# One over the root mean square by a single power instruction on GpSimd in a two-layer attention encoder

## The chip, the cores and the metric

The kernel runs on one core of one Trainium2 chip. The metric is the device time of one execution in microseconds (us). Before the change it is 863.17 us, the median of three runs (861.14 to 863.44).

## What is computed

The reference runs two layers over 512 tokens of 1024 features, in float32. Each layer normalises its input by the root mean square, projects it, mixes tokens by attention, multiplies by a gate and projects back onto the residual. What matters here is the normalisation, which is used in two forms: over the 1024 features of a token, and over the 64 features of each head of q and k.

```python
def rms_norm(x, g):
    xf = x.astype(jnp.float32)
    y = xf * lax.rsqrt(jnp.mean(xf * xf, axis=-1, keepdims=True) + RMS_EPS)
    return (y * g.astype(jnp.float32)).astype(x.dtype)

# layer A (dilated windows), for each of 3 groups:
q = rms_norm(qkv[:, :, g, 0], q_gain[g]); k = rms_norm(qkv[:, :, g, 1], k_gain[g])
# layer B (neighbourhood on a grid):
q = rms_norm(q.reshape(b, s, N_HEADS, HEAD_DIM), q_gain) * (HEAD_DIM ** -0.5)
k = rms_norm(k.reshape(b, s, N_HEADS, HEAD_DIM), k_gain)
```

So every place needs `(mean + eps) ** -0.5`, for 4 values per partition (tokens) or 16 or 32 values per partition (heads of a tile of tokens).

## The kernel before, in words

**Work and order.** The 16 heads are handled in 8 pairs (`hc` 0 to 7), first for layer A, then for layer B, with an output projection after each layer. Weights stream from HBM in tiles of 512 or 384 columns. Every weight tile is split into a high part `wh` (a cast on ScalarE, `split`, L127) and a low part `wl` (a subtraction, L131, on VectorE for three tiles of five and on GpSimd for two of five, L128 to L131). TensorE then makes three matmuls for each product: high by high, high by low, low by high. A tile's halves have four buffers each and are made up to four tiles ahead. TensorE's instructions stand in a hand-written order: the main sequence of projections (`main`) is mixed with a side sequence (`side`) of attention work by a clock that adds up the length of the matmuls, and waits such as `yield "wait", ("rawq", hc), 15000` say how much later than the projection the transposes of q may come. The order on the other engines is found by the framework's scheduler from its own simulated times; each engine runs its instructions strictly in that order.

**The norm of the heads.** In layer A the projection of k for two groups gives `rawk` (four token tiles of 512 columns, of which 256 are k: 16 heads' sums per partition) and that of q gives `rawq` (four token tiles of 512 columns, three groups of q and one of k: 32 sums per partition). In layer B one projection gives q, k and v at once (16 sums per partition). Each token tile is evicted from PSUM by ScalarE with the token's factor `rs_n` (L428), squared on GpSimd (`squares`, L268) and summed on VectorE (L269). Then `head_norm` calls `rsqrt`, on VectorE when there are 32 sums (q of layer A, 8 times) and on GpSimd when there are 16 (k of layer A and all of layer B, 16 times). The result `rs` multiplies the tile on VectorE (L284, four instructions). This scaling is issued at once for k of layer A and for q of its last two pairs; in the other cases it is held back in `later` until after the gate's first multiplication (`gate_a` L458, `main_b` L899). After it TensorE transposes q and k (L210).

**The norm of the tokens.** `row_scale` calls `rsqrt` on VectorE with 4 sums per partition, which come from PSUM, once in each layer. The result `rs_n` is the scale of the evictions that follow and is spread over a tile by TensorE (`spread`).

**`rsqrt`.** It works out `v = ss * scale + EPS` (L108), makes a first guess of the inverse root by integer arithmetic on the bits (L109), and takes three Newton steps. On VectorE a step has three instructions (L113, L115, L116), on GpSimd four (L113, L118, L119, L120). So a call has 11 instructions on VectorE and 14 on GpSimd. The buffer `v` has one instance, `a` two.

Of the kernel before, what the change touches and what calls it, by code (L numbers as in the profile page):

```python
# [13 lines left out]
F32 = mybir.dt.float32  # L14
F32R = mybir.dt.float32r
I32 = mybir.dt.int32
AF = mybir.ActivationFunctionType
ALU = mybir.AluOpType
# [4 lines left out]
P = 128  # L23
# [19 lines left out]
def tile_hybrid_encoder(  # L43
# [13 lines left out]
    nc = tc.nc  # L57
    ctx.enter_context(tc.manual_schedule(engines={mybir.EngineType.PE}))

    cp = ctx.enter_context(tc.tile_pool(name="cp", bufs=1))  # L60
    big = ctx.enter_context(tc.tile_pool(name="big", bufs=1))
    wp = ctx.enter_context(tc.tile_pool(name="wp", bufs=3))
    wk = ctx.enter_context(tc.tile_pool(name="wk", bufs=2))
# [31 lines left out]
    lb_d = dr.tile([P, 376], F32, name="lb_d")  # L95
    gb_d = dr.tile([P, 248], F32, name="gb_d")

    v0 = [cp.tile([P, 4, P], F32, name=f"v0_{i}") for i in range(2)]

    hn_h = big.tile([P, KT, S], F32R, name="hn_h")  # L100
# [2 lines left out]
    y_l = big.tile([P, KT, S], F32R, name="y_l")  # L103

    def rsqrt(eng, r, ss, n, scale):
        v = wk.tile([P, 32], F32, tag="nv", name="nv", bufs=1)
        a = wk.tile([P, 32], F32, tag="na", name="na")
        eng.tensor_scalar(v[:, :n], ss, scale, EPS, op0=ALU.mult, op1=ALU.add)  # L108
        eng.tensor_scalar(  # L109
            r.bitcast(I32), v[:, :n].bitcast(I32), -0.5, float(0x5F3759DF), op0=ALU.mult, op1=ALU.add  # L110
        )
        for _ in range(3):
            eng.tensor_mul(a[:, :n], r, r)  # L113
            if eng is nc.vector:
                eng.scalar_tensor_tensor(a[:, :n], a[:, :n], -0.5, v[:, :n], op0=ALU.mult, op1=ALU.mult)  # L115
                eng.scalar_tensor_tensor(r, a[:, :n], 1.5, r, op0=ALU.add, op1=ALU.mult)  # L116
                continue
            eng.tensor_mul(a[:, :n], a[:, :n], v[:, :n])  # L118
            eng.tensor_scalar(a[:, :n], a[:, :n], -0.5, 1.5, op0=ALU.mult, op1=ALU.add)  # L119
            eng.tensor_mul(r, r, a[:, :n])  # L120

    turn, pool = [0], [2, 5]

# [151 lines left out]
    def head_norm(raw, ss, ns, held):  # L275


        rs = wk.tile([P, 32], F32, tag="rs", name="rs")
        rsqrt(nc.vector if ns == 8 else nc.gpsimd, rs[:, : 4 * ns], ss[:, : 4 * ns], 4 * ns, 1.0 / DH)

        def scale():
            for i in range(4):
                v = raw[:, i, : ns * 64].rearrange("p (a b) -> p a b", b=64)
                m = nc.vector.tensor_mul(  # L284
                    v, v, rs[:, i * ns : (i + 1) * ns].unsqueeze(2).to_broadcast([P, ns, 64])
                )
                if held:
                    tc.keep_in_program_order(m)

        if held:  # L290
            later.append(scale)
        else:
            scale()
# [33 lines left out]
    def row_scale(ssq):  # L327

        rsqrt(nc.vector, rs_n, ssq, 4, 1.0 / D)
# [854 lines left out]
```

## Time and profile before

| | before |
|---|---|
| median of 3 runs | 863.17 us |
| the profiled execution | 863.44 us |
| its span, first to last instruction | 861.7 us |
| TensorE clock granted | 0.999 |
| DMA, mean over the span | 149 GB/s |
| ScalarE (ACT) busy | 423.1 us (49%) |
| L284, the scaling of q and k on VectorE, with `rawq` | 32 instructions, median 684 ns |
| L428, the eviction of `rawq` on ScalarE | 32 instructions, median 690 ns |

A profile row of a group names the line of the kernel, the engine, the operation, what it writes and reads, and its count, then its busy time in us and the mean of one in ns, and then the idle time of its engine ahead of it with what ended that idle time. PE is TensorE, PEld its loading of weights, DVE VectorE, ACT ScalarE, POOL GpSimd, SP the engine that issues the DMAs. In a view by tile the three durations are the shortest, the median and the longest in ns. In a timeline the first column is the start in us from the beginning of the span, the second the duration in us.

### The profile page before, as it was taken

The numbers are of one execution on the slowest core, as the hardware profiler recorded it, in microseconds if no ns is written. First come the engines' busy times: TensorE is split into PE (matmuls) and PEld (weight loads), VectorE is DVE, ScalarE is ACT, GpSimd is POOL, SyncE is SP. The second block draws the span as 40 slices with busy tenths as digits, with TensorE's granted clock in tenths as the row PEclk, the third lists the DMA queues.
The fourth block names the chain that finished last, engine by engine and source line by source line (L and its number), as shares of the span: only waits on it lengthen the run. The fifth ranks groups of instructions, "written<-read, shape, count | busy, mean of one in ns | idle before, by whom it ended". The sixth has DMA issues, their size and how long they took to land.

```text
span 861.7 us, 15492 instructions
## 1 busy us (share of the span) xinstructions
PE 854.2 (99%) x5643; PEld 712.2 (83%) x5643; DVE 513.3 (60%) x1323; ACT 423.1 (49%) x880; POOL 296.2 (34%) x493
## 2 busy tenths in 40 slices
PE   8999999999999999999999999999999999999998
PEld 6788888788788788788788788789988899889786
DVE  6445666566476566566466775538466656766642
ACT  7432653553553553553552564435466645665541
POOL 2351441441541432442342432112444335542411
PEclk9999999999999999999999999999999999999999
DMA  7343565564465464465465274265235664656223
GB/s 247 110 131 108 150 170 157 159 178 137 138 202 156 125 200 130 133 192 148 129 171 175 84 229 105 65 197 179 95 113 149 180 168 145 167 160 174 99 96 124
DMA packets 59707, 128.64 MB, mean 149 GB/s; under 512 B 6384, under 2 KB 23728, under 8 KB 59632
## 3 DMA queue, kind: packets, MB, share of 16 engines
q1 hardware_dynamic: 59344, 127.66, 49.3%
q8 instruction: 44, 0.72, 0.4%
q14 instruction: 31, 0.25, 0.1%
q10 hardware_dynamic: 288, 0.01, 0.0%
HBM read 102.82 MB, written 24.83 MB: 148 GB/s over the span
## 4 chain that ended last, share of the span: by engine, by line
PE 97%; ACT 1%; DVE 1%; DMA 1%; issue 0%; ACTq 0%; DVEq 0%
PE acc L206 82%; PE log L206 5%; PE o L206 5%; PE tp L210 4%; DMA hg<-in_head_gain 1%; ACT p L976 1%; DVE hn_l L368 0%; ACT p L564 0%; ACT rawk L428 0%; ACT wh L127 0%; PE pa L206 0%; PE pl L206 0%; PE pk L206 0%; DVE wl L131 0%; DVE pt L889 0%
## 5 line engine op out<-in xcount | busy, mean ns | idle before, releaser
L127 ACT CAST wh<-wraw 128x512 fp32r<-128x512 f32 (+1 forms) x276 | 161.6, 587 | 298.1 <-PE acc L206 247.4
L206 PE MATMUL acc<-wh,hn_h 128*128 128x512 f32 (+1 forms) x768 | 296.5, 386 | 0.8 <-ACT wh L127 0.7
L206 PE MATMUL acc<-wh,hn_l 128*128 128x512 f32 (+1 forms) x768 | 286.6, 373 | 0.0
L206 PE MATMUL acc<-wl,hn_h 128*128 128x512 f32 (+1 forms) x768 | 286.1, 373 | 0.4 <-DVE wl L131 0.4
L131 POOL TENSOR_TENSOR wl<-wraw,wh 128x512 fp32r<-128x512 f32 (+1 forms) x110 | 137.7, 1252 | 392.9 <-ACT wh L127 342.2
L131 DVE TENSOR_TENSOR wl<-wraw,wh 128x512 fp32r<-128x512 f32 (+1 forms) x166 | 113.2, 682 | 141.5 <-ACT wh L127 137.0
L206 PEld LDWEIGHTS acc<-wh,hn_h 128*128 128x128 f32 x768 | 144.6, 188 | 27.4 <-issue 5.5
L206 PEld LDWEIGHTS acc<-wh,hn_l 128*128 128x128 f32 x768 | 144.6, 188 | 21.1
L206 PEld LDWEIGHTS acc<-wl,hn_h 128*128 128x128 f32 x768 | 144.9, 189 | 19.0 <-DVE wl L131 0.9
L206 PE MATMUL acc<-hn_h,wh 128*128 128x512 f32 x192 | 76.9, 400 | 0.2
L206 PE MATMUL acc<-hn_h,wl 128*128 128x512 f32 x192 | 74.9, 390 | 0.0
L206 PE MATMUL acc<-hn_l,wh 128*128 128x512 f32 x192 | 74.8, 390 | 0.0
L725 ACT ACTIVATE p<-p,mn 128x512 f32<-128x512 f32 (+1 forms) x64 | 44.8, 700 | 53.9 <-DVE mn L714 53.9
L564 ACT ACTIVATE p<-p,mn 128x512 f32<-128x512 f32 (+3 forms) x128 | 69.1, 586 | 0.0
L269 DVE TENSOR_REDUCE ss<-sq 128x4 f32<-128x256 f32 (+1 forms) x96 | 48.4, 504 | 27.3 <-POOL sq L268 26.8
L636 DVE STREAM_TRANSPOSE tr<-p 128x512 f32<-128x512 f32 (+1 forms) x80 | 54.1, 688 | 12.1 <-ACT p L564 10.0
L268 POOL TENSOR_TENSOR sq<-rawk 128x256 f32<-128x256 f32 x64 | 40.5, 640 | 40.5 <-ACT rawk L428 33.5
L206 PE MATMUL acc<-y_h,wh 128*128 128x512 f32 x128 | 52.2, 408 | 0.0
L206 PE MATMUL acc<-y_h,wl 128*128 128x512 f32 x128 | 50.0, 390 | 0.0
L206 PE MATMUL acc<-y_l,wh 128*128 128x512 f32 x128 | 50.0, 390 | 0.0
L206 PEld LDWEIGHTS acc<-hn_h,wh 128*128 128x128 f32 x192 | 36.1, 188 | 9.8 <-ACT rawk L428 2.1
L206 PEld LDWEIGHTS acc<-hn_h,wl 128*128 128x128 f32 x192 | 36.0, 188 | 7.7
(131 smaller groups left out, 1077.8 us busy)
## 6 DMA issues: line engine op xcount, KB each, us to landing
wraw<-in_w SPq DMA_DIRECT2D x95, 512.0 KB
wraw<-in_w SPq DMA_DIRECT2D x38, 384.0 KB
td<-tr SPq DMA_DIRECT2D x56, 256.0 KB
pt<-td SPq DMA_DIRECT2D x56, 256.0 KB
td<-tr SPq DMA_DIRECT2D x24, 224.0 KB
pt<-td SPq DMA_DIRECT2D x24, 224.0 KB
e<-l_d SPq DMA_DIRECT2D x32, 112.0 KB
e<-l_d SPq DMA_DIRECT2D x16, 128.0 KB
```

The source lines that it names most:

```text
L127: nc.scalar.copy(h, raw)
L131: eng.tensor_sub(l, raw, h.bitcast(F32))
L206: nc.tensor.matmul(o, l, r, **kw)
L210: nc.tensor.transpose(o, i, ident)
L268: nc.gpsimd.tensor_mul(sq, raw[:, i, : ns * 64], raw[:, i, : ns * 64])
L269: nc.vector.tensor_reduce(ss[:, i * ns : (i + 1) * ns], sq.rearrange("p (a b) -> p a b", b=64), axis=AX.X, op=ALU.add)
L564: nc.scalar.activation(pr, pr, AF.Copy, scale=mn[:, 3:4])
L636: nc.vector.transpose(dst, src[:, :n].rearrange("p (i b k) -> p i b k", b=4, k=32))
L725: nc.scalar.activation(row, row, AF.Exp, bias=mn[:, 1:2], scale=-1.0, accum_out=mn[:, 2:3])
L976: nc.scalar.activation(pr[:, o : o + n], pr[:, o : o + n], AF.Exp, bias=mn[:, 0:1], scale=-1.0, accum_out=mn[:, 2:3])
```

## The change

`rsqrt` keeps its first instruction on the engine that it had (VectorE or GpSimd). The guess and the Newton steps go, and one instruction takes their place, on GpSimd in all 26 calls: a tensor raised to the power that a second tensor holds, which is a constant tile of -0.5. That tile is filled once at the start by VectorE. The buffer `a` goes, and `v` has two instances now.

```diff
+    neg = cp.tile([P, 32], F32, name="neg")
+    nc.vector.memset(neg, -0.5)
...
     def rsqrt(eng, r, ss, n, scale):
-        v = wk.tile([P, 32], F32, tag="nv", name="nv", bufs=1)
-        a = wk.tile([P, 32], F32, tag="na", name="na")
+        v = wk.tile([P, 32], F32, tag="nv", name="nv")
         eng.tensor_scalar(v[:, :n], ss, scale, EPS, op0=ALU.mult, op1=ALU.add)
-        eng.tensor_scalar(
-            r.bitcast(I32), v[:, :n].bitcast(I32), -0.5, float(0x5F3759DF), op0=ALU.mult, op1=ALU.add
-        )
-        for _ in range(3):
-            eng.tensor_mul(a[:, :n], r, r)
-            if eng is nc.vector:
-                eng.scalar_tensor_tensor(a[:, :n], a[:, :n], -0.5, v[:, :n], op0=ALU.mult, op1=ALU.mult)
-                eng.scalar_tensor_tensor(r, a[:, :n], 1.5, r, op0=ALU.add, op1=ALU.mult)
-                continue
-            eng.tensor_mul(a[:, :n], a[:, :n], v[:, :n])
-            eng.tensor_scalar(a[:, :n], a[:, :n], -0.5, 1.5, op0=ALU.mult, op1=ALU.add)
-            eng.tensor_mul(r, r, a[:, :n])
+        nc.gpsimd.tensor_tensor(r, v[:, :n], neg[:, :n], op=ALU.pow)
```

## The prediction, made before the result was known

> **What bounds the kernel.** I read the page's head first, then the chain that ended last, then the waits of TensorE.
>
> ```profile
> span 861.7 us, 15492 instructions
> PE 854.2 (99%) x5643; PEld 712.2 (83%) x5643; DVE 513.3 (60%) x1323; ACT 423.1 (49%) x880; POOL 296.2 (34%) x493
> ...
> PE 97%; ACT 1%; DVE 1%; DMA 1%; issue 0%; ACTq 0%; DVEq 0%
> ```
>
> TensorE is busy for 854.2 of 861.7 us and 97% of the last chain is its own. So 7.5 us at most could be had by making other engines quicker. The view of the waits, asked for TensorE alone, says how much of that ended with a late producer:
>
> ```profile
> PE busy L346 <- DVE warm L335: 1.5, 1, 1.5
> PE acc L206 <- ACT wh L127: 0.7, 1, 0.7
> PE acc L206 <- DVE wl L131: 0.4, 1, 0.4
> PE tp L210 <- ACT p L564: 0.4, 1, 0.4
> PE o L206 <- issue: 0.3, 1, 0.3
> ```
>
> None of the rows names `rs` or `rs_n`. The norm is therefore off the path now, and the whole question is how late its result may become before TensorE stands still for it.
>
> **What goes.** The view by tile of `na` shows the removed steps (shortest/median/longest in ns):
>
> ```profile
> L113 POOL TENSOR_TENSOR na<-rs x48: 216/217/667, 44.4 to 804.0; 128x16 f32<-128x16 f32 x48
> L118 POOL TENSOR_TENSOR na<-na,nv x48: 217/223/550, 44.7 to 804.3; 128x16 f32<-128x16 f32 x48
> L119 POOL TENSOR_SCALAR na<-na x48: 203/205/688, 45.0 to 804.6; 128x16 f32<-128x16 f32 x48
> L120 POOL TENSOR_TENSOR rs<-rs,na x48: 222/223/768, 45.3 to 804.9; 128x16 f32<-128x16 f32 x48
> L115 DVE SCALAR_TENSOR_TENSOR na<-na,nv x30: 155/192/1271, 36.3 to 604.5; 128x32 f32<-128x32 f32 x24, 128x4 f32<-128x4 f32 x6
> ```
>
> On GpSimd 16 calls lose 13 of their 14 instructions, 192 of them in these rows: 48 x (217+223+205+223) ns = 41.7 us busy at the medians. On VectorE 8 calls lose ten instructions of about 0.19 us each, some 15 us at the medians, and two calls ten shorter ones. Neither engine is the bound (60% and 34% busy), so this time is worth nothing by itself.
>
> **What comes: the price of the power.** The trace has no power instruction. The nearest below is a GpSimd multiplication of the same size, 217 ns for 16 columns (L113). The nearest in width is this row of the view by tile of `sq`:
>
> ```profile
> L268 POOL TENSOR_TENSOR sq<-rawq x32: 1032/1042/1061, 55.3 to 488.2; 128x512 f32<-128x512 f32 x32
> ```
>
> From 16 to 512 columns the time grows by 825 ns, that is 1.66 ns a column, and 0.19 us stay fixed. A power needs a logarithm, a product and an exponential. I count some 80 elementary steps (an estimate from the arithmetic, no row shows it). Three prices follow:
> - floor: 0.22 us for 16 columns, as one multiplication; with the columns' growth 0.25 us for 32;
> - chosen: 80 steps at 1.66 ns, 0.133 us a column with 0.19 us fixed: 0.7 us for 4 columns, 2.3 us for 16, 4.4 us for 32;
> - ceiling: every step costs as much per column as a whole separate instruction of 16 columns does, 217/16 = 13.6 ns: 1.09 us a column, 17.5 us for 16 and 34.9 us for 32.
>
> I take the middle value because the power is one instruction whose steps run without a start between them, so that the wide row is the nearer one. The choice is weak, and the ends lie far apart.
>
> **Where it stands: q of layer A (8 calls, 32 columns).** Timelines of VectorE, GpSimd and TensorE around pair 1:
>
> ```profile
> 126.10 0.22 DVE L108 TENSOR_SCALAR nv<-ss 128x32 f32<-128x32 f32 x1
> ...
> 128.16 1.27 DVE L115 SCALAR_TENSOR_TENSOR na<-na,nv 128x32 f32<-128x32 f32 x1
> 129.46 0.19 DVE L116 SCALAR_TENSOR_TENSOR rs<-na,rs 128x32 f32<-128x32 f32 x1
> 130.34 0.69 DVE L458 TENSOR_TENSOR gt<-acc,rs_half 128x512 f32<-128x512 f32 x1 [0.68 <-PE acc L206]
> 130.94 2.49 DVE L284 TENSOR_TENSOR rawq<-rawq,rs 128x512 f32<-128x512 f32 x4
> ...
> 128.09 1.29 POOL L131 TENSOR_TENSOR wl<-wraw,wh 128x512 fp32r<-128x512 f32 x1 [1.81 <-ACT wh L127]
> ...
> 135.58 0.60 PE L210 MATMUL tp<-ident,rawq 128*128 128x128 f32 x4
> 136.25 0.40 PE L206 MATMUL acc<-wl,hn_h 128*128 128x512 f32 x1
> ```
>
> Now `rs` is ready at 129.65, but the scaling is held behind the gate's product until 130.94 and takes 2.49 us, and TensorE transposes at 135.58. `rs` may thus come as late as 135.58 - 2.49 = 133.09. With the change the first instruction ends at 126.32, some 0.1 us pass on the way to the other engine (as between 604.87 and 604.96 in a fence below; taken between the two instructions everywhere), and the power runs from 126.42 to 130.8: still ahead of 130.94. The cover is 133.09 - 126.42 = 6.7 us, so this place turns at a price of 0.2 us a column. What queues behind the power is the GpSimd subtraction of 128.09, moved to 130.8 and ended by 132.1, against its use by TensorE at 136.25: also covered. In pair 6 the scaling isn't held back, and less is covered:
>
> ```profile
> 456.17 0.22 DVE L108 TENSOR_SCALAR nv<-ss 128x32 f32<-128x32 f32 x1
> ...
> 459.75 2.50 DVE L284 TENSOR_TENSOR rawq<-rawq,rs 128x512 f32<-128x512 f32 x4
> ...
> 463.61 0.60 PE L210 MATMUL tp<-ident,rawq 128*128 128x128 f32 x4
> ```
>
> Here 463.61 - 2.50 - 456.49 = 4.6 us are covered, just over the 4.4 us that I take. VectorE waits there with the scaling in its queue, and its next subtraction follows 1.1 us later.
>
> The row of 1.27 us above is a step whose median is 0.19 us: it began while the GpSimd subtraction of 128.09 ran, and ended with it. So a VectorE instruction with two inputs in SBUF stands still while GpSimd reads. The Trainium skill says the same in "SBUF — State Buffer", section "SBUF: two separate sides": the pair of ports that the two engines share is locked for a whole instruction. The trace agrees (0.19 became 1.27 us). By that rule a power of 4.4 us blocks VectorE's two-input work for all of it. In pair 1 only the gate's product stands there, and one of its inputs is in PSUM, so the sum stays; it speaks against the change only where the power is long.
>
> **k of layer A and layer B (16 calls, 16 columns).** Timelines of k in pair 1, then of pair 2 in layer B:
>
> ```profile
> 96.91 0.21 POOL L108 TENSOR_SCALAR nv<-ss 128x16 f32<-128x16 f32 x1 [0.96 <-DVE ss L269]
> ...
> 97.97 1.29 POOL L131 TENSOR_TENSOR wl<-wraw,wh 128x512 fp32r<-128x512 f32 x1
> ...
> 102.68 1.43 DVE L284 TENSOR_TENSOR rawk<-rawk,rs 128x256 f32<-128x256 f32 x4 [1.30 <-POOL rs L120]
> ...
> 107.65 0.39 PE L206 MATMUL acc<-wl,hn_h 128*128 128x512 f32 x1
> 112.19 0.38 PE L210 MATMUL tp<-ident,rawk 128*128 128x128 f32 x2
> ```
>
> ```profile
> 662.73 0.20 POOL L108 TENSOR_SCALAR nv<-ss 128x16 f32<-128x16 f32 x1
> ...
> 668.73 2.23 DVE L284 TENSOR_TENSOR rawk<-rawk,rs 128x256 f32<-128x256 f32 x4 [0.72 <-POOL rs L120]
> ...
> 671.91 0.60 PE L210 MATMUL tp<-ident,rawk 128*128 128x128 f32 x4
> ```
>
> In both the chain of 14 steps lasts nearly 6 us, because a subtraction or a `y_l` slips in between its steps. With the power it lasts 0.3 + 2.3 = 2.6 us, about 3 us less, and VectorE's waits of 1.30 and 0.72 us for `rs` go. TensorE gains nothing: its transposes come at their place in the order. The covers are 112.19 - 1.43 - 97.2 = 13.5 us for k, 107.65 - 1.29 - 97.2 = 9.1 us for the subtraction that queues behind the power, and 671.91 - 2.23 - 663.03 = 6.65 us in layer B.
>
> **The tokens' norm (2 calls, 4 columns) and the constant.** At the start of layer B:
>
> ```profile
> 601.87 0.16 DVE L108 TENSOR_SCALAR nv<-pk 128x4 f32<-128x4 f32 x1 [1.48 <-PE pk L206]
> ...
> 604.71 0.16 DVE L116 SCALAR_TENSOR_TENSOR rs_n<-na,rs_n 128x4 f32<-128x4 f32 x1
> 604.96 2.00 ACT L428 ACTIVATE rawk<-acc,rs_n 128x384 f32<-128x384 f32 x4 [0.31 <-DVE rs_n L116]
> ```
>
> The chain of 3.0 us becomes 0.16 + 0.1 + 0.7 us, or some 2 us if a GpSimd subtraction of 1.3 us is ahead of it. This brings the evictions forward by about 1 us, ahead of matmuls that already run. I count nothing. The constant is one small fill at the start, while TensorE only waits for its first weights: nothing.
>
> **Sum.** Zero on the path, with perhaps half a microsecond of the small waits recovered: 863.4 - 0.2 = 863.2 us, from the profiled execution's 863.44 us (span 861.7 and 1.7 around it), which is also about the median of the runs, 863.17.
>
> **Rivals.**
> 1. *The power is slow* because its steps wait for one another. Its prices begin at 0.2 us a column, where q of pair 1 starts to lose (1.5 times what I chose), and end here at 0.38, the geometric mean of my price and the ceiling. At that end a power takes 6.3 us for 16 columns and 12.35 for 32. Layer B and k stay covered (6.65, 9.1). q loses 12.35 - 6.67 = 5.7 us in seven pairs (0 and 7 taken like pair 1) and 7.7 in pair 6: 47.5 us, 911 us at the far end, 866 to 911 for the case. For it: 80 steps that need each other's results sit in one instruction. Against it: the wide multiplication shows no such cost, though its columns don't need each other. The Trainium skill, "GPSIMD Engine Reference", section "Performance pitfalls for Q7 kernels", prices a dependent float32 chain at 4 cycles an element on the chain; no run here shows it. At the page's 1.2 GHz an estimate from it is 80 x 4 cycles = 0.27 us a column, 8.7 us for 32 columns, and 7 x 2.1 + 4.1 = 19 us, 882 us.
> 2. *Dearer than that, up to the ceiling*, as if the values were taken one after another: at the ceiling q loses 7 x 28.2 + 30.3 = 228 us, k 8 x (17.5 - 9.1) = 67 by the subtraction behind it, layer B 8 x 10.85 = 87: 382 us, 1245 us. For it: the trace shows no power at all. Against it: no GpSimd row here pays anew for every column.
> 3. *A new wait in GpSimd's queue at my price*: if the power of q is ordered behind the subtraction of 128.09, which itself waits for ScalarE, it ends at 129.4 + 4.4 = 133.8, 0.7 us too late, in seven pairs; in pair 6 3.0 us too late. 8 us, 871 us. It decides once that subtraction comes first. For it: GpSimd was idle for 1.81 us ahead of it, so the order is open. Against it: the power is ready 1.7 us before it.
> 4. *Faster*: the waits of the rows above that could end, 0.7 + 0.4 + 0.4 us, go: 861.9 us. More than 0.3% (2.6 us) would need a third of all TensorE's idle time.
>
> **Chances.** My forecast 0.44, rival 1 0.27, rival 2 0.15, rival 3 0.10, rival 4 0.04. 0.3% is about what a measurement of this kernel can tell from no change. So: faster 0.04, within 0.3% 0.44, slower 0.52. The slower ones together hold more than the forecast, which is only the likeliest single case; its own range is 861 to 866. The range of 861 to 912 adds rivals 1 and 3 and leaves out rival 2 and the ends of the others, some 2 in 10.
>
> **What would show it.** Right: a power of about 2.3 us for 16 columns and 4.4 us for 32, twice what 16 take but for the fixed part; the scaling of q starting after the gate's product as now; no row of TensorE waiting for VectorE's `rawq`. VectorE's busy time falls by some 20 us, and GpSimd's rises by some 28: 16 x 2.3 + 8 x 4.4 + 2 x 0.7 = 73 us come, 45 go with guess and steps. Wrong: a power over 6.7 us for 32 columns, with idle TensorE ahead of the transposes of `rawq` in each pair of layer A, then of layer B, or GpSimd's `wl` late.

## The result, and the profile after

The changed kernel takes 873.06 us (median, 872.62 to 875.25), against 862.75 us for the kernel before on the same chip. The ratio is 1.0127 with a 95% interval from 1.0104 to 1.015: slower by 9 to 13 us. The time lies in the range that was given, but not where the forecast put it.

The head of the page of the kernel after, and the chain that ended last:

```profile
span 870.9 us, 15207 instructions
PE 857.4 (98%) x5643; PEld 712.7 (82%) x5643; DVE 503.2 (58%) x1224; ACT 424.1 (49%) x880; POOL 338.2 (39%) x311
...
PE 90%; DVE 5%; ACT 2%; DMA 2%; POOL 1%; issue 1%; ACTq 0%; SPq 0%; DVEq 0%; POOLq 0%
```

The chain, 97% TensorE before, now runs for 5% of the span over VectorE. The waits of TensorE in the kernel after say where:

```profile
PE tp L201 <- DVE rawq L275: 4.5, 13, 1.3
PE tp L201 <- DVE mn L705: 2.2, 1, 2.2
```

Both rows are new: the transposes of q (L201, L210 before) wait for the scaling of q (L275, L284 before) 13 times, and once for the softmax. In the view by tile of `nv` stands what could not be seen before, the power itself:

```profile
L111 POOL TENSOR_TENSOR rs<-nv,neg x24: 2898/2902/5458, 42.3 to 810.5; 128x16 f32<-128x16 f32 x16, 128x32 f32<-128x32 f32 x8
L111 POOL TENSOR_TENSOR rs_n<-nv,neg x2: 1014/1020/1026, 34.1 to 612.5; 128x4 f32<-128x4 f32 x2
```

It takes 1.02 us for 4 columns, 2.90 for 16 and about 5.44 for 32: 0.16 us a column and some 0.38 us fixed.

TensorE's 5643 matmuls stand in the same order in all kernels here, so the start of each can be set against its start in the kernel before. The table has how much later TensorE is after each stretch than ahead of it, from the profiled executions, in us. "Pair" is the attention of that pair of heads in layer A.

| kernel | pair 0 | pairs 1 to 5, each | pair 6 | pair 7 | rest |
|---|---|---|---|---|---|
| after | 0.0 | 0.92 to 0.94 | 2.77 | 3.99 | -0.1 |
| e1_newton_q | 0.0 | 0.0 | 0.0 | -0.1 | -0.3 |
| e2_pow_q_only | 0.0 | 0.95 to 1.25 | 4.34 | 2.38 | -0.3 |
| e3_moved | 0.0 | 0.0 | 0.60 | 1.31 | -0.2 |
| e4_newton_pool | 0.0 | 0.0 | 0.61 | 1.76 | -0.4 |
| e5_moved_twice | 6.40 | 5.7 to 5.8 | 7.86 | 7.49 | 0.1 |
| e6_pieces | 0.7 | 0.0 | 0.52 | 1.56 | 0.6 |
| e7_before_moved | 0.0 | 0.0 | 0.0 | 0.0 | -0.1 |

All of the loss is at q of layer A, in pairs 1 to 7: 11.4 us by the sum of the row. The first 30 us are left out of the table, since they differ from execution to execution: the kernel after is 1.87 us earlier there than the profiled execution of before, and so is e4_newton_pool, which has no power, by 1.91 us. That is why the spans differ by 9.2 us only. A row is one execution; that of e4_newton_pool was its fastest of five (863.27 us, median 865.05).

Pair 1 in the timelines of the kernel after, VectorE first, then GpSimd, then TensorE:

```profile
124.22 0.22 DVE L110 TENSOR_SCALAR nv<-ss 128x32 f32<-128x32 f32 x1
128.45 0.69 DVE L449 TENSOR_TENSOR gt<-acc,rs_half 128x512 f32<-128x512 f32 x1 [4.01 <-PE acc L197]
129.06 0.68 DVE L122 TENSOR_TENSOR wl<-wraw,wh 128x512 fp32r<-128x512 f32 x1
...
130.18 4.69 DVE L275 TENSOR_TENSOR rawq<-rawq,rs 128x512 f32<-128x512 f32 x4
...
124.52 5.44 POOL L111 TENSOR_TENSOR rs<-nv,neg 128x32 f32<-128x32 f32 x1
129.92 1.50 POOL L122 TENSOR_TENSOR wl<-wraw,wh 128x512 fp32r<-128x512 f32 x1
131.91 1.81 POOL L122 TENSOR_TENSOR wl<-wraw,wh 128x512 fp32r<-128x512 f32 x1 [0.49 <-ACT wh L118]
...
133.69 0.38 PE L201 MATMUL tp<-ident,rawq 128*128 128x128 f32 x2
134.33 0.33 PE L201 MATMUL tp<-ident,rawq 128*128 128x128 f32 x1 [0.25 <-DVE rawq L275]
134.93 0.33 PE L201 MATMUL tp<-ident,rawq 128*128 128x128 f32 x1 [0.28 <-DVE rawq L275]
```

The power ends at 129.96, and the scaling starts at 130.18, 3.51 us ahead of the first transpose, where it was 4.64 us ahead before (135.58 - 130.94). After scalings of 2.49 us there were 2.15 us left over; the power's length takes 1.1 of them, and the rest would do. But the four scalings last 4.69 us where they lasted 2.49. While the power ran, a GpSimd subtraction became due (ScalarE's cast for it began at 125.50) and had to wait; it starts at 129.92, the next follows at 131.91, and both run while q is scaled. Only the first of them was held up. In the kernel before, the second is this row:

```profile
133.80 1.38 POOL L131 TENSOR_TENSOR wl<-wraw,wh 128x512 fp32r<-128x512 f32 x1 [4.42 <-ACT wh L127]
```

It starts 1.78 us ahead of the first transpose there (135.58 - 133.80) and in the kernel after (133.69 - 131.91). Before, the scaling was over by then; now it runs later and into it. Each of the two stretches the scaling that it meets. The view by tile of `rawq` has the longest one:

```profile
L275 DVE TENSOR_TENSOR rawq<-rawq,rs x32: 677/680/1787, 66.9 to 504.9; 128x512 f32<-128x512 f32 x32
```

Two of four scalings take 1.78 us instead of 0.68: 2.2 us more. With the 1.1 us of above that is more than was left over, by 1.2 us. The last scaling is needed only by the fourth transpose, so 0.9 us are lost. Of the 2.15 us, the lateness alone leaves about half, and the collisions alone would leave about nothing (an estimate from these rows): by it the loss takes both together.

### The profile page after: what moved, and what is told of

It reads as the page before. It is cut to its first block, busy times and chain, and to the rows that moved or that the text cites. A ratio compares the mean times of both kernels' runs of the same rounds, so it can differ in the third digit from the quotient of the medians.

```text
span 870.9 us, 15207 instructions
## 1 busy us (share of the span) xinstructions
PE 857.4 (98%) x5643; PEld 712.7 (82%) x5643; DVE 503.2 (58%) x1224; ACT 424.1 (49%) x880; POOL 338.2 (39%) x311
## 4 chain that ended last, share of the span: by engine, by line
PE 90%; DVE 5%; ACT 2%; DMA 2%; POOL 1%; issue 1%; ACTq 0%; SPq 0%; DVEq 0%; POOLq 0%
PE acc L197 75%; PE log L197 5%; PE o L197 5%; PE tp L201 4%; DVE rawq L275 3%; POOL rs L111 1%; DMA td<-tr 1%; DMA pt<-td 1%; ACT p L967 1%; DMA hg<-in_head_gain 0%; DVE gt L449 0%; DVE hn_l L359 0%; ACT eg L452 0%; ACT p L555 0%; ACT rawk L419 0%
## 5 line engine op out<-in xcount | busy, mean ns | idle before, releaser
L122 POOL TENSOR_TENSOR wl<-wraw,wh 128x512 fp32r<-128x512 f32 (+1 forms) x110 | 140.3, 1275 | 387.5 <-ACT wh L118 323.4
L111 POOL TENSOR_TENSOR rs<-nv,neg 128x16 f32<-128x16 f32 (+1 forms) x24 | 90.2, 3759 | 4.0 <-DVE nv L110 1.9
L275 DVE TENSOR_TENSOR rawk<-rawk,rs 128x256 f32<-128x256 f32 x64 | 33.1, 577 | 20.1 <-POOL rs L111 20.1
```

The lines of the kernel that those rows point to most:

```text
L111: nc.gpsimd.tensor_tensor(r, v[:, :n], neg[:, :n], op=ALU.pow)
L122: eng.tensor_sub(l, raw, h.bitcast(F32))
L275: m = nc.vector.tensor_mul(v, v, rs[:, i * ns : (i + 1) * ns].unsqueeze(2).to_broadcast([P, ns, 64]))
```

## The experiments

Theory A: the power of q ends in time, or nearly, but it pushes two GpSimd subtractions into the scaling of q, and the ports that the two engines share do the damage. (By the rows above it pushes one, and the later scaling runs into the other.) Theory B: the power is simply late for q. Theory C: long instructions in GpSimd's queue cost everywhere. Theories D, L and M came with later runs and are told there.

**Newton steps for q alone.** The edit to the kernel before, in `rsqrt`, besides the constant tile (the guess and the Newton steps stay below it; `v` and `a` have one buffer each):

```diff
-        a = wk.tile([P, 32], F32, tag="na", name="na")
         eng.tensor_scalar(v[:, :n], ss, scale, EPS, op0=ALU.mult, op1=ALU.add)
+        if n < 32:
+            nc.gpsimd.tensor_tensor(r, v[:, :n], neg[:, :n], op=ALU.pow)
+            return
+        a = wk.tile([P, 32], F32, tag="na", name="na", bufs=1)
```

> The power stays for k of layer A, for layer B and for the tokens (16 and 4 columns); q of layer A (32 columns) has its Newton steps on VectorE back. Theory A (the power of q ends in time, but pushes two GpSimd subtractions into the scaling of q, where the shared ports stretch it): the whole loss goes, 861 to 865 us, ratio to before 0.998 to 1.002, scaling of q 2.5 us for four. Theory B (the power itself is late for q): the same here, 861 to 865. Theory C (any long instruction in GpSimd's queue costs, whatever its size): the 16 remaining powers of 2.9 us keep half of the loss or more, 867 to 870.

Measured: 861.17 us against 861.87, ratio 0.9996 (0.9986 to 1.0005). The 16 powers for k and for layer B, and the two for the tokens, cost nothing and bring nothing. Theory C falls.

**The power for q alone.** The same edit with `if n == 32`.

> The power for q of layer A alone; all other places keep guess and Newton steps. Theories A and B: the whole loss is here, 871 to 875 us, with about 0.96 us lost in each of pairs 1 to 5 and 2.5 to 4 in pairs 6 and 7. Theory C: a third to a half of it, 866 to 869.

Measured: 874.43 us, ratio 1.0138 (1.0122 to 1.0154). The whole loss is here, with nearly the same share in each of pairs 1 to 5. Pair 6 loses more than was expected (4.34 us) and pair 7 less (2.38), where the kernel after has 2.77 and 3.99. Two rows of a view by windows, one behind the transposes of each pair, show why (after the stretch: its length, the busy times of PE, PEld, DVE, ACT and POOL, then the granted clock of TensorE):

```profile
472.30:475.80 3.50, 3.50 (x12) 2.81 (x11) 0.81 (x2) 0.96 (x2) 0.00 (x0) 0.51 0.00 0
511.20:513.20 2.00, 2.00 (x13) 1.78 (x14) 1.90 (x10) 2.00 (x6) 0.00 (x0) 1.00 0.06 17
```

Behind pair 6 the clock is at half, which costs 1.6 us against the kernel after (4.34 - 2.77); behind pair 7 it stays at 1.00. In the kernel after it is pair 7 that meets the half clock, as is shown further down.

**The subtractions out of the way.** In `split` of the kernel after:

```diff
+        to_pool = to_pool and turn[0] - 1 not in {22, 42, 44, 62, 64, 82, 84, 102, 104, 122, 124, 142, 144, 152}
         eng = nc.gpsimd if to_pool else nc.vector
```

> As after the change, but the 14 subtractions that ran on GpSimd during the scaling of q are given to VectorE, so that nothing on GpSimd reads while q is scaled. The power and the time at which it is ready stay. Theory A: the four scalings take 2.5 us again instead of 4.7, pairs 1 to 5 lose nothing, pair 6 loses 0.5 to 1 and pair 7 2 to 4 (its power is waited for with the softmax behind it): 864 to 868 us. Theory B: the power is as late as before, so nothing changes: 872 to 875. Theory C: 870 or more.

Measured: 863.27 us against 861.87, ratio 1.0017 (1.0008 to 1.0026), just below the range that theory A gave (pair 7 loses 1.31 us where 2 to 4 were expected). Pair 1 in its timelines:

```profile
130.29 2.49 DVE L276 TENSOR_TENSOR rawq<-rawq,rs 128x512 f32<-128x512 f32 x4
...
124.63 5.44 POOL L111 TENSOR_TENSOR rs<-nv,neg 128x32 f32<-128x32 f32 x1
...
133.80 0.60 PE L202 MATMUL tp<-ident,rawq 128*128 128x128 f32 x4
```

The power takes 5.44 us as in the kernel after, and the scaling starts 3.51 us ahead of the first transpose, as there. It takes 2.49 us again, and TensorE's four transposes go through in a row. Pairs 1 to 5 lose nothing. Theory B falls for them: the lateness alone costs nothing there. What is left, 0.60 and 1.31 us in pairs 6 and 7, can't be the collision and is lateness.

**Short instructions in place of the long one.** The kernel before, with q's guess and Newton steps on GpSimd:

```diff
-        rsqrt(nc.vector if ns == 8 else nc.gpsimd, rs[:, : 4 * ns], ss[:, : 4 * ns], 4 * ns, 1.0 / DH)
+        rsqrt(nc.gpsimd, rs[:, : 4 * ns], ss[:, : 4 * ns], 4 * ns, 1.0 / DH)
```

> As before the change, but q's guess and Newton steps are on GpSimd (14 short instructions of 32 columns in place of one long one; no power at all). They last 4.3 us or more, and one GpSimd subtraction is ordered between them, so rs comes later than from the power. Theory A: that subtraction is done before the scaling, so at most one subtraction meets the scaling: pairs 1 to 5 lose 0 to 0.7 us, 863 to 869 us in all. Theory B: rs is later than the power's, so the loss is as large or larger: 872 to 880. Theory C (one long instruction): no loss, 862 to 865.

Measured: 865.05 us, ratio 1.0035 (1.0018 to 1.0052). Its timelines of GpSimd and VectorE in pair 1:

```profile
126.19 1.28 POOL L131 TENSOR_TENSOR wl<-wraw,wh 128x512 fp32r<-128x512 f32 x1 [0.30 <-ACT wh L127]
...
129.03 0.81 POOL L120 TENSOR_TENSOR rs<-rs,na 128x32 f32<-128x32 f32 x1
...
129.87 2.50 DVE L284 TENSOR_TENSOR rawq<-rawq,rs 128x512 f32<-128x512 f32 x4
```

The expectation that `rs` would come later was wrong: it is ready at 129.84, within 0.12 us of the power's 129.96. So the two kernels can be compared closely, though the scaling starts 0.3 us earlier here, since VectorE's gate product of 129.84 is ordered behind it. With nearly the same ready time, the subtraction slips in between the steps at 126.19, is over long before the scaling, and pairs 1 to 5 lose nothing. What hurts there is not the lateness alone but that one instruction of 5.4 us lets nothing through.

**The cover.** As e3_moved, with q's power done twice, so that its result comes 5.44 us later:

```diff
         nc.gpsimd.tensor_tensor(r, v[:, :n], neg[:, :n], op=ALU.pow)
+        if n == 32:
+            nc.gpsimd.tensor_tensor(r, v[:, :n], neg[:, :n], op=ALU.pow)
```

> As e3_moved (nothing on GpSimd reads while q is scaled), and q's power is done twice over, so that rs is ready 10.9 us after the power's start instead of 5.44. Theory A with the cover of the prediction (6.67 us in pair 1, 4.62 in pair 6): pairs 1 to 5 lose 10.88 - 6.67 = 4.2 us each, pairs 6 and 7 each 5.4 us more than the 0.6 and 1.3 that they lose in e3_moved, pair 0 2 to 3: 35 us in all above before, 893 to 900 us. Theory D (the length of the power adds to the time in full, with no cover): 8 x 5.44 = 44 us more than e3_moved, 905 to 909.

Measured: 912.23 us against 862.87, ratio 1.0567 (1.0542 to 1.0591), which is neither theory's. Pair 1, in the timelines of VectorE and TensorE and in two rows of a view by windows:

```profile
143.60 2.50 DVE L278 TENSOR_TENSOR rawq<-rawq,rs 128x512 f32<-128x512 f32 x4 [0.30 <-POOL rs L113]
...
147.12 0.63 PE L200 MATMUL acc<-wh,hn_h 128*128 128x512 f32 x1
147.55 0.63 PE L200 MATMUL acc<-wl,hn_h 128*128 128x512 f32 x1
...
138.00:144.00 6.00, 3.86 (x18) 2.85 (x16) 2.06 (x4) 1.24 (x2) 5.52 (x1) 1.00 1.05 244
...
148.20:150.20 2.00, 2.00 (x8) 1.60 (x8) 0.00 (x0) 0.69 (x1) 0.00 (x0) 0.50 0.00 0
```

Until the fourth transpose TensorE loses 4.1 us in this pair, where the cover gave 4.2. Then the granted clock falls to 0.50, the matmuls of 512 columns start 0.43 us apart instead of 0.23, and another 1.7 us go. So the cover was right, and a second cost came with the idle time. Pair 0, for which 2 to 3 us were expected, loses 6.40. Its windows:

```profile
75.20:79.20 4.00, 3.47 (x10) 2.35 (x10) 2.50 (x5) 1.20 (x2) 0.00 (x0) 0.50 0.00 0
79.20:82.00 2.80, 2.80 (x10) 2.31 (x9) 1.31 (x2) 0.69 (x2) 0.00 (x0) 0.50 0.25 76
```

Here the stretch at half clock is 6.8 us long and costs half of that, 3.4 us. The 3.0 us that are left are the lateness, as expected. The half clock, which theory A didn't count, is most of what lies above its 893 to 900 us.

**The power in pieces.** As the kernel after, with q's power in four pieces of 8 columns, each issued behind the sums of its own token tile (the call in `head_norm` stays for 16 columns alone, and `rs` is made earlier):

```diff
             squares(raw, ss, i, ns)
+            if ns == 8:
+                rsqrt(nc.vector, rs[:, 8 * i : 8 * i + 8], ss[:, 8 * i : 8 * i + 8], 8, 1.0 / DH)
```

> As after the change, but q's power is done in four pieces of 8 columns, each as soon as its token tile's sums are there. GpSimd spends more time on powers than with one of 32 columns (4 x 1.66 = 6.6 us against 5.44), but no subtraction waits behind 5.44 us; the last piece is ordered behind the subtraction that comes ahead of the scaling. Theory A: pairs 1 to 5 lose 0 to 0.6 us each (the last piece ends about 1 us after the gate's product, and one subtraction may meet the scaling), pairs 6 and 7 together 1 to 3: 863 to 869 us. Theory D (GpSimd's time in powers is what costs): 874 us or more.

Measured: 865.12 us, ratio 1.0025 (1.0014 to 1.0036). The view by tile of `nv`:

```profile
L111 POOL TENSOR_TENSOR rs<-nv,neg x48: 1629/1643/3212, 44.0 to 804.1; 128x8 f32<-128x8 f32 x32, 128x16 f32<-128x16 f32 x16
```

GpSimd spends 4 x 1.64 = 6.6 us on q's powers instead of 5.44, and pairs 1 to 5 lose nothing. The time in powers is not the cost.

**Control.** The kernel before, with the edit of e3_moved in `split`.

> Control: before the change, with the same 14 subtractions given to VectorE as in e3_moved. Theory A: they cost nothing and bring nothing where they are (no q scaling met them, but for one in pair 7): 861 to 863.5 us, ratio 0.998 to 1.001. If moving them were a gain by itself, 860 or less, and e3_moved would not show the collision alone.

Measured: 862.97 us against 862.87, ratio 0.9999 (0.999 to 1.0008). Moving the subtractions is worth nothing by itself.

**Wider powers beside VectorE.** As the kernel after, with powers of 1, 8, 64 and 128 columns at the start that nobody reads.

> As after the change, with four more powers on a scratch tile at the start, of 1, 8, 64 and 128 columns, whose results nobody reads. From the powers of 4, 16 and 32 columns (1.02, 2.90, 5.44 us): 0.16 us a column and 0.38 us fixed, so about 0.5, 1.7, 10.6 and 20.9 us. The long ones run beside VectorE instructions with two inputs in SBUF (the sums of squares and the low parts of x). Theory L (a GpSimd instruction keeps the shared ports for all its length): such instructions last up to the power's length. Theory M (the power reads only now and then, or early): they keep their 0.7 us, as the subtractions inside the powers of 5.44 us did. The time of this kernel says nothing, since the first weights wait behind the powers: some 20 to 30 us longer.

One execution, 887.41 us; the time is not compared. The view by tile of `po`, then GpSimd's and VectorE's timelines:

```profile
L341 POOL TENSOR_TENSOR po<-pw x4: 570/6104/21229, 1.9 to 17.8; 128x1 f32<-128x1 f32 x1, 128x8 f32<-128x8 f32 x1, 128x64 f32<-128x64 f32 x1, 128x128 f32<-128x128 f32 x1
...
17.81 21.23 POOL L341 TENSOR_TENSOR po<-pw 128x128 f32<-128x128 f32 x1
...
14.94 1.76 DVE L122 TENSOR_TENSOR wl<-wraw,wh 128x512 fp32r<-128x512 f32 x1
...
19.84 2.27 DVE L1052 TENSOR_TENSOR x_all<-x_all 128x512 f32<-128x512 f32 x3
22.03 0.68 DVE L122 TENSOR_TENSOR wl<-wraw,wh 128x512 fp32r<-128x512 f32 x1
```

The power of 128 columns runs from 17.81 to 39.04. Inside it three sums with two inputs in SBUF take 2.27 us together and a subtraction 0.68 us, close to the median of 0.68 that both have in the kernel before. The subtraction of 14.94 met a GpSimd subtraction instead and took 1.76 us. Theory L falls. Theory M's durations came; when the power reads, no run shows.

## Why the prediction was right in its range and wrong in its forecast

**Right.** TensorE is the bound, and the covers that were worked out hold, each taken alone: in pair 1 the power ends inside its cover of 6.7 us (5.44), k and layer B lose nothing (e1_newton_q, 0.9996), and the cover of q held when it was tried (4.1 us lost against 4.2). The tokens' norm and the constant cost nothing. Nothing was gained either, as said. One reading beside it did not come: VectorE's waits for the `rs` of k and layer B did not go but rose in sum, from 15.4 us to 20.1, since its scaling is ordered earlier; they cost TensorE nothing.

**The step that failed** is the one on what queues behind the power. It moved the GpSimd subtraction from 128.09 to 130.8 and ended it by 132.1, and found it covered, because TensorE needs it only at 136.25. It did not ask what else runs between 130.8 and 132.1: the scaling of q, from 130.94, two inputs in SBUF. Even at the price that was taken the subtraction would have landed in it. The rule that was weighed further down, and the row of 1.27 us beside it, are just this collision; the step turned them on the power ("blocks VectorE's two-input work for all of it. [...] so the sum stays") and not on the subtraction that the power moves. The runs show the opposite: the power blocks nothing, the subtraction does, and the scaling that it delays meets the next one too. That is 2 x 1.1 us in pairs 1 to 5, of which, with the lateness of 1.1 us, 0.9 us reach TensorE. e3_moved, without collisions, and e4_newton_pool, with the subtraction let through, both lose nothing there. The step also asked of each effect by itself whether it was covered, while all of them draw on the same cover.

That the time lies between 861 and 912 us is luck as far as the cause goes: the range reached so high for a dearer power and for another order in GpSimd's queue, and neither came.

**Sizes.** The power costs 0.16 us a column against 0.133, 1.2 times as much: 5.44 us for 32 columns against 4.4. The 0.133 was 80 steps, a count that no run shows, times 1.66 ns of a multiplication; which of the two was too small stays open. In pairs 1 to 5 the extra 1.0 us is nearly all of the 1.1 us by which the scaling starts later, and so it matters. No run has the collisions without this lateness. By the durations above they come to 2.2 us against the 2.15 left over, so by this estimate a power of 4.4 us would have lost next to nothing there, collisions and all. In pair 6 it passes the cover of 4.62 us by 0.8 us, and 0.60 us are lost there without any collision. GpSimd's busy time rose by 42.0 us, not 28 (its powers take 92 us, not 73), and VectorE's fell by 10.1, not 20; the stretched scalings work against it.

**Pair 7 was taken like pair 1, and isn't.** Its scaling isn't held back, and the softmax of other scores stands behind it on VectorE. GpSimd, VectorE, TensorE of the kernel after there, and its windows:

```profile
496.60 5.43 POOL L111 TENSOR_TENSOR rs<-nv,neg 128x32 f32<-128x32 f32 x1
...
502.06 3.56 DVE L275 TENSOR_TENSOR rawq<-rawq,rs 128x512 f32<-128x512 f32 x4 [4.44 <-POOL rs L111]
...
507.42 0.63 PE L201 MATMUL tp<-ident,rawq 128*128 128x128 f32 x4 [2.22 <-DVE mn L705]
...
505.20:507.40 2.20, 0.00 (x0) 0.01 (x1) 2.20 (x12) 0.09 (x1) 0.00 (x0) 1.00 0.68 151
507.40:509.20 1.80, 1.78 (x10) 1.61 (x11) 1.80 (x9) 1.80 (x6) 0.00 (x0) 0.82 0.02 8
509.20:511.20 2.00, 2.00 (x9) 1.60 (x8) 0.88 (x3) 2.00 (x7) 0.00 (x0) 0.50 0.82 236
```

VectorE waits 4.44 us for the power, one collision takes 1.1 us (one did before, too, where the four scalings took 3.59 us), the softmax comes late, and the transpose waits for it: 2.2 us idle. Without the collision, in e3_moved, 1.1 us are idle. Then the clock is at 0.50 and takes 1.6 us more, which e2_pow_q_only, just as late here, doesn't lose (2.38 us against 3.99). This is a wait with a queue behind it, as rival 3 had it, but on VectorE and not on GpSimd.

**The rivals.** Rival 1 did not come: its price begins at 0.2 us a column. Rival 2 is far off. Rival 3 named 8 us and 871 us, near to what was measured, by another way: the power was not ordered behind the subtraction but ahead of it. In e6_pieces the last piece is ordered behind it, and pairs 1 to 5 lose nothing there.

What stays open: when a short idle time is followed by the half clock, and how much the collisions would cost without the lateness.

## What to carry to other kernels

When one long instruction takes the place of many short ones on an in-order queue, ask what came through between the short ones and where it will run now: its lateness may be covered, and its new neighbours still not. Count all that draws on one cover together. List for each instruction that is moved which instructions of the other engine it now overlaps, two inputs in SBUF on both sides first. Where slack is counted in a place that repeats, count it again in each place whose order differs (first, last, not held back).

## What the runs showed of the hardware

- **A power on GpSimd** costs about 0.16 us a column: 0.57 us for 1 column, 1.64 for 8, 2.90 for 16, 5.44 for 32, 21.23 for 128.
- **It does not hold up VectorE.** The Trainium skill, "SBUF — State Buffer", section "SBUF: two separate sides", says that the shared ports are locked for a whole instruction. For GpSimd's subtraction the runs agree (0.68 us became 1.78 on VectorE). For the power they don't: VectorE's subtraction at 129.06, 4.5 us into the power, took 0.68 us, and so did the one inside the power of 21.23 us.
- **The clock of TensorE can halve after a short idle time, and need not.** After 2.2 us of idling in pair 7 of the kernel after it is granted 0.50 for some 3.4 us, which costs 1.6 us; the same 2.2 us in e2_pow_q_only bring no such stretch. In pair 6 it is the other way round: e2_pow_q_only has the stretch, where 1.34 us is the longest of its waits, and the kernel after, with the same waits, has not. So the length of the wait alone does not decide it. The Trainium skill, "TensorE: Matmul & The Clock Gate", section "Part 1: The HAM clock gate", has the half rate follow an idle window of about 3.4 us; the runs show it after less.
